# A two-layer decoder trunk: a bank of its own for the last half product, the other accumulator copied in late pairs, and the first forget weights split early with their product behind the transposes

## The chip, the cores and the metric

The kernel runs on one core of one Trainium2 chip. The metric is the device time of one execution in microseconds; lower is better. Before the change it was 1370.78 us (median of three runs, 1370.76 to 1370.94).

## The reference

A residual stream x of 1024 tokens by 1024 channels (float32) passes through two layers, and a final RMSNorm ends the trunk. Each layer is, shortened,

```python
h = rms_norm(x, norm_w[layer])
proj = h @ w_in[layer]
(q, k, v, z_attn, q_h, f_h, i_h, g_h, gate_attn, gate_hgrn) = jnp.split(proj, split_points, axis=-1)
a = sliding_window_attention(rope(q), rope(k), v, attn_sinks[layer]) * jax.nn.silu(z_attn)
logf = jnp.log(lb + (1.0 - lb) * jax.nn.sigmoid(f_h))
kin = (1.0 - lb) * jax.nn.sigmoid(-f_h)
o = hgrn2_recurrence(silu(q_h), kin, i_h, logf)
b = rms_norm_per_head(o) * jax.nn.silu(g_h)
merged = (jax.nn.sigmoid(gate_attn) * (a @ w_up_attn[layer])
          + jax.nn.sigmoid(gate_hgrn) * (b @ w_up_hgrn[layer]))
x = x + merged @ w_out[layer]
```

The attention has 8 heads of 64 channels (two key and value heads), a window of 128 tokens and one sink logit per head; the recurrence has 4 heads of 128 channels, and its forget gate is the sigmoid of f_h. Everything is float32.

## The kernel before

**Products.** A float32 product is made of three matmuls on split operands: each operand is split into a rounded high part and the rest (names hh, hl for the activations; wh or whi, wl or wlo for weights), and low by high, high by low and high by high are summed in one bank of PSUM. A weight is split by ACT (a cast, the high part) and DVE (a subtraction, the low part): `split_slot` (L463 to L472) and `split_w` (L135 to L139). PSUM has eight banks: three for the accumulators of projections and pairs (pool `pj`), five for the rest (pool `ps`, function `bank`). A matmul that opens a bank waits until the bank's last reader is done.

**Order.** Each engine runs its own queue in order, and waits for other engines through semaphores. The order within a queue is set when the kernel is built: a list scheduler takes the program's instructions and reorders them by its own estimates, unless an instruction is marked with `keep_in_program_order` or stands in a region of `manual_schedule`, where the program's order holds. The end of the last layer (function `end`) is such a region.

**The stage around the forget gate.** Attention is worked in eight blocks of 128 tokens. For step u the program calls `before(u)`, `value(u)` and `attend(u)`. `scores(b)` makes block b's scores on TensorE (tiles sc, four banks a block; ACT copies the masked half out, L837, DVE masks it, L838, and takes row maxima, L840). `softmax(b)` takes exponentials on ACT (L853, eight a block) and normalises on DVE (L856). `turn(b)` transposes the probabilities on TensorE (tiles tp, two banks of four transposes a block, L865); ACT copies each (L869) and DVE multiplies each by a mask (L870), both into pT. `values` multiplies pT by the values (tiles av, L889) for two blocks at a time; every one of these matmuls is made to wait (`wait_too`) for the DVE copies of both blocks. ACT copies av out (L882). After block 7's `value`, `forget(0, ...)` computes head 0 of the forget projection in two halves of 512 tokens, H0 and H1: 24 matmuls each into a bank of `pj` (tiles pj_f, L148 to L150, function `proj3`), and then two sigmoids and two scalings on ACT (L776 and L778), for which ACT loads another function table, and two DMAs from ACT's queue. In program order the forget product of H0 comes behind block 6's scores and ahead of block 7's, and that of H1 behind the transposes of blocks 4 and 5.

**Pairs.** `pair` makes two column groups of the input projection at once from half products, in the accumulators A, B and C. Fifteen pairs are made in each layer. For the last ones (three in the first layer, four in the second) there is no first product p1 from an earlier stage, and results are copied out of a bank by ACT and completed by sums on DVE.

**The end.** The output projection of the last layer is made of seven half products, summed by DVE into x (L1372). The last one, with the operands t2 (split as w4), adds to the banks X[0] to X[3] for row blocks 4 to 7, block 7 in two halves of 256 columns. A row block is done when its final RMSNorm is: ACT squares and sums (L1374), DVE and ACT take mean and root (L1378 to L1393), DVE scales (`scaled`, L1401), or DVE multiplies by the norm's gain early (`weigh`, L1406) and ACT scales later (`scaled_weighed`, L1410), and a DMA from SP's queue stores the block's half.

Of the kernel before, what the change touches and what calls it, by code (L numbers as in the profile page):

```python
# [17 lines left out]
P = 128  # L18
# [23 lines left out]
def trunk_kernel(ctx, tc, x, positions, norm_w, w_in, attn_sinks, hgrn_norm_w, w_up_attn,  # L42
# [101 lines left out]

    def proj3(acc, terms):
        n = len(terms)
        for i, (lh, ll, rh, rl) in enumerate(terms):
            PE.matmul(acc, lhsT=ll, rhs=rh, start=i == 0, stop=False)  # L148
            PE.matmul(acc, lhsT=lh, rhs=rl, start=False, stop=False)  # L149
            PE.matmul(acc, lhsT=lh, rhs=rh, start=False, stop=i == n - 1)  # L150
# [215 lines left out]
    def pair(w, cols, parts, hT, nm, p1, use):  # L366
# [61 lines left out]
        o22 = out("22")  # L428
        if p1 is not None:
            add(o22, C, p1)  # L430
        times(B, h1[:, 0], l1[:, 0], part(2), False)
        if p1 is not None:
            add(o22, B, o22)
        else:
            S.copy(o22, B)  # L435
            add(o22, C, o22)
        use(1, 1, o22, True)
# [10 lines left out]

    def colsA(wh, wl, hT, nm, use, groups):

        for a, o, n in groups:
            acc = pj.tile([P, n], F32, tag="pj", name=f"pj_{nm}_{a}_{o}")
            terms = []
            for k in range(KT):
                h, l = hT.half(a, k)
                terms.append((wh[:, k], wl[:, k], h[:, o:o + n], l[:, o:o + n]))
            proj3(acc, terms)
            use(a, slice(o, o + n), slice(a * 512 + o, a * 512 + o + n), acc)
# [144 lines left out]
    for L in range(DEPTH):  # L603
# [177 lines left out]
        def forget(h, w, groups):  # L781
            def use(a, o, t, acc):
                put(h, 0, t, acc, AF.Sigmoid, 1.0, lb[:, L, h:h + 1])
                put(h, 1, t, acc, AF.Sigmoid, -1.0, 0.0)
            colsA(w[0], w[1], hT, f"f{L}_{h}", use, groups)

# [144 lines left out]
        for u in range(NB):  # L931
            before(u)
            value(u)
            attend(u)
            if u == 5:
                w = [split_slot(load_chunk(wi, OF, f"f{L}_0"), f"f{L}_0", [P, KT, P])]
        w.append(chunk(wi, OQH, f"qh{L}_0"))
        for u in range(4):
# [426 lines left out]

        def add(acc, a, n, js=range(4), c=None, part=None):

            for j in js:
                b = 4 * a + j
                o, k = c or (0, 512)  # L1370
                xn = xns[b][:, n * 512 + o:n * 512 + o + k]
                V.tensor_tensor(out=xn, in0=acc[j][:, o:o + k], in1=xn, op=ALU.add)  # L1372
                if part is not None:
                    S.activation(junk[:, n * 512 + o:n * 512 + o + k], xn, AF.Square, scale=D ** -0.5,  # L1374
                                 accum_out=fs[:, part, b:b + 1])
# [31 lines left out]

        def scaled_weighed(b, n):
            t, _, d = piece(b, n)
            S.activation(t, t, AF.Copy, scale=fy[:, b:b + 1])  # L1410
            nc.sync.dma_start(d, t)

        def end():

            one = [slice(b, b + 1) for b in range(NB)]
            add(Y, 0, 1, part=1)
            w4 = split_a(t2, "t4")
            mean(slice(0, 4), 0, 1)
            square_root(slice(0, 4))
            root(slice(0, 4), 4)  # L1420
            for j in range(4):
                scaled(j, 0)
                add(X, 1, 1, [j], part=1)
                scaled(j, 1)
            weigh(4, 1)

            def last_product(j, o, n):
                for kp in range(2):
                    times(X[j][:, o:o + n], m22[kp], [t[:, :, o:o + n] for t in w4[kp]], j, False, kp)

            last_product(0, 0, 512)
            add(X, 1, 0, [0], part=0)
            weigh(5, 1)
            mean(one[4], 0, 1)
            square_root(one[4])
            last_product(1, 0, 512)
            add(X, 1, 0, [1], part=0)
            root(one[4], 1)
            scaled(4, 0)
            scaled_weighed(4, 1)  # L1440
            weigh(6, 1)
            mean(one[5], 0, 1)
            square_root(one[5])
            last_product(2, 0, 512)
            add(X, 1, 0, [2], part=0)
            root(one[5], 1)
            scaled(5, 0)
            scaled_weighed(5, 1)
            weigh(7, 1)
            mean(one[6], 0, 1)  # L1450
            square_root(one[6])
            last_product(3, 0, 256)
            add(X, 1, 0, [3], (0, 256), part=0)
            root(one[6], 1)
            V.tensor_tensor(out=fs[:, 1, one[7]], in0=fs[:, 0, one[7]], in1=fs[:, 1, one[7]], op=ALU.add)
            last_product(3, 256, 256)
            add(X, 1, 0, [3], (256, 256), part=2)
            scaled(6, 0)
            mean(one[7], 1, 2)
            square_root(one[7])  # L1460
            scaled_weighed(6, 1)
            root(one[7], 1)
            scaled_weighed(7, 1)
            scaled(7, 0)
# [97 lines left out]
```

## Time and profile before

| | us |
|---|---|
| median of three runs | 1370.78 |
| the profiled execution's own time | 1372.09 |
| its span, first to last instruction | 1370.3 |
| PE (TensorE) busy | 1354.8 |
| DVE (VectorE) busy | 974.3 |
| ACT (ScalarE) busy | 721.2 |

The profile is of one execution. A row of a timeline gives start, duration, engine, line, operation, what is written and read, shapes and count, and in brackets the idle time ahead of it and who ended it. Matmuls overlap: a matmul of 128x512 is shown with 0.39 us, while its successor starts 0.23 us later; so the pace is read from starts. Rows of waits give the waiting engine and line, the engine and line waited for, and total, count and longest in us.

### The profile page before, as it was taken

The page shows a single profiled execution, that of the slowest core. Times are in us where ns is not written, and L with a number is a line of the kernel's source. Part 1 is how long each engine was busy: PE and PEld are TensorE (multiplying, and loading weights), DVE is VectorE, ACT ScalarE, POOL GpSimd, SP SyncE. Part 2 cuts the span into 40 slices and gives each one's busy share as a digit, 9 for nine tenths or more (in the row PEclk, how much of TensorE's full clock was granted, in tenths as well). Part 3 has the DMA queues.
Part 4 walks back from the last instruction along what each step waited for, and adds up shares of the span by engine and source line. Part 5 has one row for each costly group of instructions (what it writes and reads, how often), then busy time and mean ns, then how long its engine had stood idle before and what let it go on. Part 6 is the DMA issues. An engine that isn't in the chain of part 4 may idle for free.

```text
span 1370.3 us, 21561 instructions
## 1 busy us (share of the span) xinstructions
PE 1354.8 (99%) x8248; PEld 1128.3 (82%) x8248; DVE 974.3 (71%) x1554; ACT 721.2 (53%) x1407; POOL 130.8 (10%) x211
## 2 busy tenths in 40 slices
PE   9999999999999999999999999999999999999997
PEld 8888888788877888888888888888887788888886
DVE  5877668843646888599758666777356388967987
ACT  7754334443786665326566333344357767552464
POOL 2000013220000011001010001122100000200100
PEclk9999999999999999999999999999999999999998
DMA  8636467876325842497255345587923376349813
GB/s 272 201 122 185 125 209 218 258 258 219 93 93 184 277 144 96 141 355 203 92 171 189 124 132 185 170 256 219 321 92 100 131 237 210 117 142 357 206 34 123
DMA packets 207559, 248.74 MB, mean 182 GB/s; under 512 B 14912, under 2 KB 141504, under 8 KB 207456
## 3 DMA queue, kind: packets, MB, share of 16 engines
q1 hardware_dynamic: 155744, 145.10, 32.9%
q0 software_dynamic: 15472, 49.43, 13.0%
q10 hardware_dynamic: 36240, 52.84, 10.7%
q8 instruction: 65, 1.06, 0.3%
q14 instruction: 38, 0.31, 0.1%
HBM read 162.12 MB, written 78.91 MB: 176 GB/s over the span
## 4 chain that ended last, share of the span: by engine, by line
PE 91%; DVE 5%; ACT 2%; DMA 1%; issue 1%; SPq 0%; ACTq 0%; DVEq 0%
PE pb L394 6%; PE pb L396 6%; PE pb L395 6%; PE pc L394 4%; PE pc L396 4%; PE pc L395 4%; PE pg L234 3%; PE pg L233 3%; PE pg L235 3%; PE pj_qh L148 2%; PE pj_f L148 2%; PE pj_f L150 2%; PE pj_qh L149 2%; PE pj_qh L150 2%; PE pj_f L149 2%; PE px L1353 2%
## 5 line engine op out<-in xcount | busy, mean ns | idle before, releaser
L137 ACT CAST whi_s<-ws 128x1024 fp32r<-128x1024 f32 x30 | 31.6, 1055 | 90.3 <-PE pc L396 90.3
L405 DVE TENSOR_TENSOR pq<-pc,pq 128x512 f32<-128x512 f32 x37 | 25.6, 691 | 62.1 <-PE pc L396 57.0
L627 ACT ACTIVATE pq<-pq 128x512 f32<-128x512 f32 x60 | 37.8, 630 | 45.3 <-DVE pq L405 43.8
L1155 POOL COPY scT<-acc 32x256 f32<-32x256 f32 x32 | 26.3, 822 | 284.3 <-DVE acc L1152 166.7
L137 ACT CAST whi_t<-ws 128x1024 fp32r<-128x1024 f32 x30 | 31.7, 1055 | 41.2 <-PE pc L396 27.3
L853 ACT ACTIVATE pr<-pr,mx 128x128 f32<-128x128 f32 x128 | 49.6, 391 | 4.1 <-DVE mx L850 3.7
L965 PE MATMUL pu_ua<-wh_a,wlo_ua 128*128 128x512 f32 x128 | 51.7, 404 | 0.0
L965 PE MATMUL pu_uh<-wh_b,wlo_uh 128*128 128x512 f32 x128 | 50.1, 391 | 0.5 <-DVE u L973 0.5
L967 PE MATMUL pu_ua<-wh_a,whi_ua 128*128 128x512 f32 x128 | 50.0, 391 | 0.0
L966 PE MATMUL pu_ua<-wl_a,whi_ua 128*128 128x512 f32 x128 | 50.0, 390 | 0.0
L967 PE MATMUL pu_uh<-wh_b,whi_uh 128*128 128x512 f32 x128 | 49.8, 389 | 0.0
L966 PE MATMUL pu_uh<-wl_b,whi_uh 128*128 128x512 f32 x128 | 49.8, 389 | 0.0
L137 ACT CAST whi_o<-wo 128x1024 fp32r<-128x1024 f32 x20 | 21.1, 1053 | 53.7 <-PE pu_uh L967 29.8
L394 PE MATMUL pb<-th,wl 128*128 128x512 f32 x120 | 47.2, 393 | 0.5 <-ACT pq L435 0.5
L394 PE MATMUL pc<-hh,wlo_t 128*128 128x512 f32 x120 | 46.9, 391 | 0.5 <-DVE pq L405 0.5
L394 PE MATMUL pb<-th,wlo_s 128*128 128x512 f32 x120 | 46.8, 390 | 0.2 <-DVE wlo_s L138 0.2
L394 PE MATMUL pb<-th,wlo_t 128*128 128x512 f32 x120 | 46.8, 390 | 0.0
L233 PE MATMUL pg<-hh,wl_p 128*128 128x512 f32 (+1 forms) x128 | 46.7, 365 | 0.0
L396 PE MATMUL pc<-hh,whi_t 128*128 128x512 f32 x120 | 46.7, 390 | 0.0
L396 PE MATMUL pb<-th,wh 128*128 128x512 f32 x120 | 46.7, 390 | 0.0
L395 PE MATMUL pb<-tl,wh 128*128 128x512 f32 x120 | 46.7, 389 | 0.0
L395 PE MATMUL pc<-hl,whi_t 128*128 128x512 f32 x120 | 46.7, 389 | 0.0
(453 smaller groups left out, 4475.2 us busy)
## 6 DMA issues: line engine op xcount, KB each, us to landing
wr<-in_w_in_dram SPq DMA_DIRECT2D x72, 512.0 KB, 4.7
gd<-pq ACTq DMA_DIRECT2D x79, 256.0 KB, 3.5
fq<-fq ACTq DMA_DIRECT2D x48, 256.0 KB, 2.9
wr_p<-in_w_in_dram SPq DMA_DIRECT2D x23, 512.0 KB, 6.3
x<-in_x_dram SPq DMA_DIRECT2D x16, 512.0 KB, 8.9
qs<-qsd POOLq DMA_DIRECT2D x16, 512.0 KB, 7.2
u<-gd SPq DMA_DIRECT2D x16, 512.0 KB, 10.2
ga<-gd SPq DMA_DIRECT2D x16, 512.0 KB, 10.6
```

The source lines that it names most:

```text
L137: S.copy(hi, raw)
L148: PE.matmul(acc, lhsT=ll, rhs=rh, start=i == 0, stop=False)
L149: PE.matmul(acc, lhsT=lh, rhs=rl, start=False, stop=False)
L150: PE.matmul(acc, lhsT=lh, rhs=rh, start=False, stop=i == n - 1)
L233: PE.matmul(acc, lhsT=wl[:, k], rhs=h[:, t], start=k == ks[0][0], stop=False, skip_group_check=q > 0)
L394: PE.matmul(acc, lhsT=wl[:, k], rhs=h, start=start and k == 0, stop=False, skip_group_check=not start)
L395: PE.matmul(acc, lhsT=wh[:, k], rhs=l, start=False, stop=False, skip_group_check=not start)
L396: PE.matmul(acc, lhsT=wh[:, k], rhs=h, start=False, stop=k == 3, skip_group_check=not start)
L853: S.activation(pr[:, h], pr[:, h], AF.Exp, bias=mx[:, h:h + 1], accum_out=sm[:, h:h + 1])
L965: PE.matmul(acc, lhsT=w[1][:, k, c], rhs=hi[:, i], start=k == 0, stop=False)
L966: PE.matmul(acc, lhsT=w[0][:, k, c], rhs=lo[:, i], start=False, stop=False)
L967: PE.matmul(acc, lhsT=w[0][:, k, c], rhs=hi[:, i], start=False, stop=k == 3)
```

## The change

Three parts.

1. In `end`, the last half product's right half of block 7 gets a bank of its own, Z, and starts it new; what was in the right half of X[3] before is added to x by a sum of its own ahead of it. The split of t2 stands first, five of the first eight `scaled` stand ahead of the sums, the `weigh` of blocks 4 to 6 are grouped, root and scale of a block change places with the sum of the next, and the last `scaled_weighed` issues its DMA from ACT's queue.
2. In `pair`, where there is no p1, ACT copies accumulator C as soon as it is done, and DVE adds B to the copy; before, ACT copied B and DVE added C.
3. The load and split of the first forget weights stand ahead of `attend(5)`, and the first matmul of each half of `forget(0, ...)` is kept in program order.

```diff
-    def proj3(acc, terms):
+    def proj3(acc, terms, pin=False):
         n = len(terms)
         for i, (lh, ll, rh, rl) in enumerate(terms):
-            PE.matmul(acc, lhsT=ll, rhs=rh, start=i == 0, stop=False)
+            mm = PE.matmul(acc, lhsT=ll, rhs=rh, start=i == 0, stop=False)
+            if pin and i == 0:
+                tc.keep_in_program_order(mm)
...
         o22 = out("22")
-        if p1 is not None:
-            add(o22, C, p1)
+        first(o22, C)
         times(B, h1[:, 0], l1[:, 0], part(2), False)
-        if p1 is not None:
-            add(o22, B, o22)
-        else:
-            S.copy(o22, B)
-            add(o22, C, o22)
+        add(o22, B, o22)
...
-            colsA(w[0], w[1], hT, f"f{L}_{h}", use, groups)
+            colsA(w[0], w[1], hT, f"f{L}_{h}", use, groups, h == 0)
...
             value(u)
-            attend(u)
             if u == 5:
                 w = [split_slot(load_chunk(wi, OF, f"f{L}_0"), f"f{L}_0", [P, KT, P])]
+            attend(u)
...
+            w4 = split_a(t2, "t4")
             add(Y, 0, 1, part=1)
-            w4 = split_a(t2, "t4")
...
+            add(X, 1, 0, [3], (256, 256))
+            Z = bank([P, 256], f"pz_{L}")
...
-            last_product(3, 0, 256)
+            last_product(X[3][:, 0:256], 3, 0, 256)
             add(X, 1, 0, [3], (0, 256), part=0)
+            mean_root(6)
+            last_product(Z, 3, 256, 256, True)
+            V.tensor_tensor(out=fs[:, 1, one[7]], in0=fs[:, 0, one[7]], in1=fs[:, 1, one[7]], op=ALU.add)
             root(one[6], 1)
-            V.tensor_tensor(out=fs[:, 1, one[7]], in0=fs[:, 0, one[7]], in1=fs[:, 1, one[7]], op=ALU.add)
-            last_product(3, 256, 256)
-            add(X, 1, 0, [3], (256, 256), part=2)
+            scaled_weighed(6, 1)
+            add([None] * 3 + [Z], 1, 0, [3], (256, 256), part=2, at=0)
             scaled(6, 0)
-            mean(one[7], 1, 2)
-            square_root(one[7])
-            scaled_weighed(6, 1)
+            mean_root(7, 1, 2)
             root(one[7], 1)
-            scaled_weighed(7, 1)
+            scaled_weighed(7, 1, nc.scalar)
             scaled(7, 0)
```

How the queues change. First TensorE's, first layer, from the transposes of blocks 2 and 3 (tp_2, tp_3) on; pj_f_0_0 is the forget product of H0, av_2 the values of block 2. Before:

```order
L865 MATMUL tp_2_0_3347<-ident,pr_2_3012 128x128 x4
L148 MATMUL pj_f_0_0_0_3486<-hh_0_0_172,wl_f_0_3267 128x512
L149 MATMUL pj_f_0_0_0_3486<-hl_0_0_180,wh_f_0_3266 128x512
...
L865 MATMUL tp_2_1_3355<-ident,pr_2_3012 128x128 x4
L865 MATMUL tp_3_0_3363<-ident,pr_3_3089 128x128 x4
L865 MATMUL tp_3_1_3371<-ident,pr_3_3089 128x128 x4
L150 MATMUL pj_f_0_0_0_3486<-hh_0_0_172,wh_f_0_3266 128x512
...
L148 MATMUL pj_f_0_0_0_3486<-hh_0_3_175,wl_f_0_3267 128x512
L889 MATMUL av_2_3407<-pT_2_0_3352,vn_2604 64x256 x2
```

and now (line numbers are those of the changed kernel):

```order
L862 MATMUL tp_2_0_3347<-ident,pr_2_3012 128x128 x4
L862 MATMUL tp_2_1_3355<-ident,pr_2_3012 128x128 x4
L862 MATMUL tp_3_0_3363<-ident,pr_3_3089 128x128 x4
L862 MATMUL tp_3_1_3371<-ident,pr_3_3089 128x128 x4
L886 MATMUL av_2_3407<-pT_2_0_3352,vn_2604 64x256 x2
...
L148 MATMUL pj_f_0_0_0_3486<-hh_0_0_172,wl_f_0_3198 128x512
L151 MATMUL pj_f_0_0_0_3486<-hl_0_0_180,wh_f_0_3197 128x512
```

Before, 5 matmuls of the forget product stood behind the first four transposes and 17 behind the others, ahead of av_2. Now av_2 follows the transposes directly, and all 24 stand behind block 6's scores. Next TensorE's queue at the transposes of blocks 4 and 5, with pj_f_0_1, the forget product of H1. Before:

```order
L833 MATMUL sc_7_1_1_3537<-ks_1_0_2805,qs_3_1_2815 128x256
L148 MATMUL pj_f_0_1_0_3600<-hhi_0_2797,wl_f_0_3267 128x512
L865 MATMUL tp_4_0_3568<-ident,pr_4_3216 128x128 x4
L149 MATMUL pj_f_0_1_0_3600<-hlo_0_2801,wh_f_0_3266 128x512
...
L150 MATMUL pj_f_0_1_0_3600<-hh_1_3_179,wh_f_0_3266 128x512
L865 MATMUL tp_4_1_3576<-ident,pr_4_3216 128x128 x4
```

and now:

```order
L830 MATMUL sc_7_1_1_3537<-ks_1_0_2805,qs_3_1_2815 128x256
L862 MATMUL tp_4_0_3568<-ident,pr_4_3222 128x128 x4
L862 MATMUL tp_4_1_3576<-ident,pr_4_3222 128x128 x4
L862 MATMUL tp_5_0_3584<-ident,pr_5_3299 128x128 x4
L862 MATMUL tp_5_1_3592<-ident,pr_5_3299 128x128 x4
L148 MATMUL pj_f_0_1_0_3600<-hhi_0_2797,wl_f_0_3198 128x512
```

The 23 forget matmuls between the first four transposes of block 4 and the next ones stand behind all of them now. Last, ACT's queue at the forget gate (fq is its result, pr_6 the probabilities of block 6, pr_7 those of block 7). Before:

```order
L837 COPY pr_6_3432<-sc_6_1_1_3449 128x2x128
L853 ACTIVATE pr_5_3299,sm_5_3464<-pr_5_3299,mx_5_3298 128x128 x3
L776 ACT_TABLE_LOAD
L776 ACTIVATE fq_0_0_0_3511<-pj_f_0_0_0_3486 128x512
...
L837 COPY pr_7_3520<-sc_7_0_0_3521 128x2x128
```

and now:

```order
L834 COPY pr_6_3432<-sc_6_1_1_3449 128x2x128
L848 ACTIVATE es_6_3553<-es_6_3553 128x8
L850 ACTIVATE pr_6_3432,sm_6_3552<-pr_6_3432,mx_6_3431 128x128 x6
L773 ACT_TABLE_LOAD
L773 ACTIVATE fq_0_0_0_3511<-pj_f_0_0_0_3486 128x512
...
L834 COPY pr_7_3520<-sc_7_0_0_3521 128x2x128
```

Six exponentials of block 6 stand ahead of the table load now, where three of block 5 stood, and the copies of block 7's scores stay behind the gate's activations. In the second layer the same orders stand.

More of the change, by code (lines that the diff above doesn't have):

```diff
@@ L447, in pair, with colsA @@
             use(1, 0, B, False)
-    def colsA(wh, wl, hT, nm, use, groups):
+    def colsA(wh, wl, hT, nm, use, groups, pin=False):
         for a, o, n in groups:
@@ L456, in colsA @@
                 terms.append((wh[:, k], wl[:, k], h[:, o:o + n], l[:, o:o + n]))
-            proj3(acc, terms)
+            proj3(acc, terms, pin)
             use(a, slice(o, o + n), slice(a * 512 + o, a * 512 + o + n), acc)
@@ L1364, in trunk_kernel, with add @@
             fm, ft, fy = (st.tile([P, NB], F32, tag=f"f{n}", name=f"f{n}", bufs=1) for n in "mty")
-        def add(acc, a, n, js=range(4), c=None, part=None):
+        def add(acc, a, n, js=range(4), c=None, part=None, at=None):
             for j in js:
@@ L1371, in add @@
                 xn = xns[b][:, n * 512 + o:n * 512 + o + k]
-                V.tensor_tensor(out=xn, in0=acc[j][:, o:o + k], in1=xn, op=ALU.add)
+                V.tensor_tensor(out=xn, in0=acc[j][:, (o if at is None else at):][:, :k], in1=xn, op=ALU.add)
                 if part is not None:
@@ L1406, in weigh, with scaled_weighed, last_product, mean_root @@
             V.tensor_tensor(out=t, in0=t, in1=w, op=ALU.mult)
-        def scaled_weighed(b, n):
+        def scaled_weighed(b, n, queue=nc.sync):
             t, _, d = piece(b, n)
             S.activation(t, t, AF.Copy, scale=fy[:, b:b + 1])
-            nc.sync.dma_start(d, t)
+            queue.dma_start(d, t)
         def end():
             one = [slice(b, b + 1) for b in range(NB)]
+            def last_product(acc, j, o, n, start=False):
+                for kp in range(2):
+                    times(acc, m22[kp], [t[:, :, o:o + n] for t in w4[kp]], j, start, kp)
+            def mean_root(b, i=0, j=1):
+                mean(one[b], i, j)
+                square_root(one[b])
+            w4 = split_a(t2, "t4")
             add(Y, 0, 1, part=1)
-            w4 = split_a(t2, "t4")
             mean(slice(0, 4), 0, 1)
@@ L1420, in end @@
             root(slice(0, 4), 4)
+            todo = [(b, n) for b in range(4) for n in range(2)]
+            for b, n in todo[:5]:
+                scaled(b, n)
             for j in range(4):
-                scaled(j, 0)
                 add(X, 1, 1, [j], part=1)
[L1424 to L1429, printed above, removed]
@@ L1431, in end @@
-            last_product(0, 0, 512)
-            add(X, 1, 0, [0], part=0)
[L1433 to L1436, printed above, removed]
-            add(X, 1, 0, [1], part=0)
[L1438 to L1444, printed above, removed]
+                for b, n in todo[5 + j:6 + j]:
+                    scaled(b, n)
@@ new lines, in end @@
+            add(X, 1, 0, [3], (256, 256))
+            Z = bank([P, 256], f"pz_{L}")
+            last_product(X[0], 0, 0, 512)
+            for b in (4, 5, 6):
+                weigh(b, 1)
+            add(X, 1, 0, [0], part=0)
+            weigh(7, 1)
+            mean_root(4)
+            last_product(X[1], 1, 0, 512)
+            root(one[4], 1)
+            scaled_weighed(4, 1)
+            scaled(4, 0)
+            add(X, 1, 0, [1], part=0)
+            mean_root(5)
+            last_product(X[2], 2, 0, 512)
@@ L1445, in end @@
+            root(one[5], 1)
+            scaled_weighed(5, 1)
             add(X, 1, 0, [2], part=0)
-            root(one[5], 1)
             scaled(5, 0)
[L1448 to L1451, printed above, removed]
-            last_product(3, 0, 256)
+            last_product(X[3][:, 0:256], 3, 0, 256)
             add(X, 1, 0, [3], (0, 256), part=0)
+            mean_root(6)
+            last_product(Z, 3, 256, 256, True)
+            V.tensor_tensor(out=fs[:, 1, one[7]], in0=fs[:, 0, one[7]], in1=fs[:, 1, one[7]], op=ALU.add)
```

## The prediction

> **What bounds the kernel now.** I read the page's busy times and the chain that ended last first.
>
> ```profile
> span 1370.3 us, 21561 instructions
> PE 1354.8 (99%) x8248; PEld 1128.3 (82%) x8248; DVE 974.3 (71%) x1554; ACT 721.2 (53%) x1407; POOL 130.8 (10%) x211
> ...
> PE 91%; DVE 5%; ACT 2%; DMA 1%; issue 1%; SPq 0%; ACTq 0%; DVEq 0%
> ```
>
> TensorE is at work for all but 15 us of the span, so a microsecond in which it waits is a microsecond of the result, and work of DVE or ACT costs only where TensorE stands for it. The view of waits, for TensorE, shows what the change can win:
>
> ```profile
> PE px L1353 <- DVE x L1372: 1.7, 1, 1.7
> ...
> PE pj_f L148 <- DVE wl_f L471: 0.9, 2, 0.4
> ...
> PE pb L394 <- ACT pq L435: 0.5, 1, 0.5
> ```
>
> These three rows are its three parts: the last half product (1.7 us, once), the first forget product (0.4 us in each layer) and the late pairs (0.5 us, once). All together some 3 us. What it can lose lies in how TensorE's queue is rearranged, above all around the forget product. The timeline of TensorE there, first layer:
>
> ```profile
> 370.08 0.66 PE L865 MATMUL tp<-ident,pr 128*128 128x128 f32 x4
> 371.18 0.50 PE L148 MATMUL pj_f<-hh,wl_f 128*128 128x512 f32 x1 [0.44 <-DVE wl_f L471]
> ...
> 372.44 1.47 PE L865 MATMUL tp<-ident,pr 128*128 128x128 f32 x12
> 373.67 0.48 PE L150 MATMUL pj_f<-hh,wh_f 128*128 128x512 f32 x1
> ...
> 377.42 0.39 PE L148 MATMUL pj_f<-hh,wl_f 128*128 128x512 f32 x1
> 377.74 0.65 PE L889 MATMUL av<-pT,vn 128*64 128x256 f32 x4
> ...
> 383.35 0.40 PE L149 MATMUL pj_f<-hl,wh_f 128*128 128x512 f32 x1
> ...
> 383.82 0.28 PE L829 MATMUL sc<-ks,qs 128*128 128x256 f32 x1
> ...
> 385.72 0.40 PE L148 MATMUL pj_f<-hhi,wl_f 128*128 128x512 f32 x1
> 385.96 0.60 PE L865 MATMUL tp<-ident,pr 128*128 128x128 f32 x4
> 386.31 0.47 PE L149 MATMUL pj_f<-hlo,wh_f 128*128 128x512 f32 x1
> ```
>
> The first column is the start; starts give the pace: 16 forget matmuls from 373.67 to 377.42, 0.23 us each; 12 transposes in 1.23 us, 0.10 each. Between the transposes of the probabilities of blocks 2 and 3 (tp) and the products that use them (av) stand 22 forget matmuls, and 23 more between the first and the other transposes of blocks 4 and 5. They are what TensorE does while DVE and ACT copy the transposes out.
>
> **The change, part by part.**
>
> *Forget product, first stall.* The split moves ahead of attend(5). DVE is free there, so this costs nothing:
>
> ```profile
> 367.86 1.25 DVE L838 COPY_PREDICATED pr<-upper,sc 128x256 f32<-128x256 int32 x3 [4.50 <-ACT pr L837]
> ...
> 369.92 1.21 DVE L471 TENSOR_TENSOR wl_f<-wr_f,wh_f 128x1024 fp32r<-128x1024 f32 x1
> 371.05 0.68 DVE L840 TENSOR_REDUCE mx<-pr 128x4 f32<-128x512 f32 x1
> ...
> 375.65 1.28 DVE L870 TENSOR_TENSOR pT<-tp,side 128x512 f32<-128x512 f32 x2
> ```
>
> The 4.50 us of idle before 367.86 take the 1.21. The stall goes: the four transposes from 370.08 need 0.41, the matmul came at 371.18, so 0.7 us per layer. And DVE's queue, which has no idle from 367.86 to 376.93, loses the 1.13 between 369.92 and 371.05: its last copy (pT of block 3) ends at 375.8.
>
> But the pin holds the whole product behind block 6's scores. TensorE now runs 16 transposes at 0.10, from 370.08 to 371.8, and then stands before av_2, which waits for that last copy: 375.9 − 371.8 = 4.1 us; I take 4.0. The bounds are 3.5 (transposes 0.5 late for their banks) and 4.3. The 22 matmuls (5 us) that covered this are not saved, they follow later.
>
> *Second stall.* From av_2 to the end of block 6's scores took 377.74 to 383.35, 5.6 us: now 375.9 to 381.5. Then 24 forget matmuls at 0.23 (5.5) to 387.0, 16 scores of block 7 (383.82 to 385.72, 1.9) to 388.9, four transposes to 389.3. The next four need the bank of block 7's first scores, so ACT's copy and DVE's mask of it. On ACT that copy stands behind the forget gate's activations:
>
> ```profile
> 375.10 0.40 ACT L853 ACTIVATE pr<-pr,mx 128x128 f32<-128x128 f32 x1 [0.36 <-DVE mx L850]
> ...
> 385.25 1.28 ACT L776 ACT_TABLE_LOAD   x1
> 386.54 1.09 ACT L776 ACTIVATE fq<-pj_f 128x512 f32<-128x512 f32 x2
> ...
> 389.34 1.20 ACT L837 COPY pr<-sc 128x256 f32<-128x256 f32 x4 [0.40 <-ACT fq L778]
> ```
>
> ```profile
> 383.04 1.25 DVE L838 COPY_PREDICATED pr<-upper,sc 128x256 f32<-128x256 int32 x3 [3.05 <-ACT pr L837]
> ...
> 386.06 0.17 DVE L841 TENSOR_TENSOR mx<-mx,sink 128x8 f32<-128x8 f32 x1
> ...
> 389.75 1.11 DVE L838 COPY_PREDICATED pr<-upper,sc 128x256 f32<-128x256 int32 x3 [2.06 <-ACT pr L837]
> ```
>
> From the table load to the first copy are 4.1 us, to DVE's mask 0.4 more, and the mask itself lasts 0.4. In the new order six exponentials of block 6 stand ahead of the load. They need DVE's maxima of block 6. The exponentials began at 375.10, behind DVE, so now at 374.0; the sixteen of blocks 4 and 5 at 0.39 and two copies of av at 0.5 last to 381.2; DVE normalises block 5 (1.2) to 382.5, and masks and maxima (3.0 from 383.04 to 386.06) with the small steps behind them (0.4) end at about 386.0. Six exponentials then end at 388.3, so the bank is free at 388.3 + 4.1 + 0.8 = 393.2. Stall: 393.2 − 389.3 = 3.9; I take 3.8. Were the exponentials never in the way, the activations would still wait for the product's end at 387.0: 2.8 from activation to copy (386.54 to 389.34) and 0.8 give 390.6, a stall of 1.3. The upper bound is 4.2. Before, 23 matmuls lay there, from 386.31 on.
>
> Per layer 4.0 + 3.8 − 0.7 = 7.1; the bounds are 4.1 (3.5 + 1.3 − 0.7) and 7.8 (4.3 + 4.2 − 0.7). For two layers **+14.2** (8.2 to 15.6).
>
> *The clock after a stall.* The kernel has one longer stall of TensorE, 1.8 us near the end. Its windows (length, busy of PE, PEld, DVE, ACT, POOL, then granted clock):
>
> ```profile
> 1360.00:1361.80 1.80, 0.08 (x2) 0.01 (x1) 1.80 (x5) 1.01 (x4) 0.00 (x0) 1.00 0.26 96
> 1361.80:1363.00 1.20, 1.20 (x10) 1.20 (x11) 0.63 (x4) 0.51 (x2) 0.00 (x0) 1.00 0.99 370
> 1363.00:1363.20 0.20, 0.20 (x4) 0.20 (x3) 0.00 (x0) 0.00 (x0) 0.00 (x0) 0.75 0.08 21
> 1363.20:1363.70 0.50, 0.50 (x3) 0.21 (x1) 0.00 (x0) 0.00 (x0) 0.00 (x0) 0.50 0.00 0
> ```
>
> After work had resumed at 1361.80 the clock fell to 0.50 at about 1363.1. Four stalls of near 4 us would each do this. How long it lasts the start shows (first matmuls, PE only):
>
> ```profile
> 1.00:2.50 1.50, 1.45 (x7) 1.00 0.40 21
> ...
> 5.50:7.00 1.50, 1.50 (x14) 1.00 0.85 252
> ```
>
> Seven matmuls in 1.5 us, later fourteen: half pace (the clock column has no record yet), which ended between 4.0 and 5.5, some 3.5 us after the first. Such a spell costs 1.75 us if TensorE works throughout it, less where part of it falls in the stall. I take 1.2 for each of four, **+4.8** (0 to 7.0).
> The Trainium skill ("TensorE: Matmul & The Clock Gate", Part 1) says the same more sharply: a free-running window of 3.4 us with TensorE idle halves the clock, and a busy one restores it. It speaks against this change; by it the stalls of 3.8 and 4.0 us are long enough to be caught and the term would be near 4 × 1.7 = 6.8, an estimate; the fall after only 1.8 us in the trace says that a window half idle is enough.
>
> *Pairs without p1* (three in the first layer, four in the second). ACT copies accumulator C instead of B, DVE adds B instead of C: as many instructions of the same shapes. What was on the path is one wait:
>
> ```profile
> 937.55 0.39 PE L394 MATMUL pb<-hh,wlo_a 128*128 128x512 f32 x1
> ...
> 937.75 0.59 ACT L435 COPY pq<-pb 128x512 f32<-128x512 f32 x1 [1.66 <-PE pb L396]
> ...
> 938.39 0.50 PE L394 MATMUL pb<-th,wl 128*128 128x512 f32 x1 [0.45 <-ACT pq L435]
> ```
>
> A matmul due at 937.78 came at 938.39: 0.6, and 0.1 of restart, so **−0.7**. The copy of C now has the 12 matmuls of B (2.7 us) as cover, and DVE's sum of B the next 12. If ACT were 2.2 us behind (0.59 of the 2.7 is the copy itself) TensorE would wait. Bounds −0.8 and +1.4 (0.2 in each of seven).
>
> *The end.*
>
> ```profile
> 1361.32 0.42 DVE L1372 TENSOR_TENSOR x<-px,x 128x256 f32<-128x256 f32 x1
> ...
> 1362.18 0.16 DVE L1393 SCALAR_TENSOR_TENSOR fy<-ft,fy 128x1 f32<-128x1 f32 x1
> ...
> 1363.74 0.42 DVE L1372 TENSOR_TENSOR x<-px,x 128x256 f32<-128x256 f32 x1 [1.21 <-PE px L1356]
> ```
>
> The right half waited for the left half's sum (1361.32), since both lay in one bank: the 1.8 us of the first window above. With its own bank it follows at once, and the sum of it, 1363.74 before, could start at about 1361.9. Now DVE is last: the left half's sum can start near 1360.2, when its product is done; fy of block 6 came 0.9 after that start (1362.18), and now ACT's square of the half, some 0.6, and its root lie between, so it comes at about 1362.1 and the bank's sum at 1362.2, 1.5 ahead of 1363.74. ACT then scales block 6 ahead of its square of the right half, which costs 0.2 to 0.3 of that; the last store has one issue fewer ahead of it on SP, since block 7's other half goes from ACT's queue, some 0.4. I take **−1.6**. Bounds: −0.3 (DVE, with one more sum of 0.42 and 1.2 of idle at 1363.74 to give up, stays as late as before) and −2.3 (the whole 1.8 and the issue).
>
> **The sum**: 14.2 + 4.8 − 0.7 − 1.6 = +16.7. The profiled execution took 1372.09 for its span of 1370.3; the runs shown have a median of 1370.78, and 16.7 on that is **1387.5**.
>
> **The rivals.**
> *The clock holds*, or its spells fall inside the stalls: 14.2 − 2.3 = +11.9, 1382.7. For it: no stall of 4 us is in this trace; against it: the fall after 1.8.
> *The second stall is short* (1.3, no fall there): per layer 4.0 + 1.3 − 0.7 = 4.6; twice, with two spells of 1.2 and −2.3 from pairs and end: +9.3, 1380.1. It needs DVE to finish block 6's maxima 2.5 earlier than I count.
> *Everything stretches*: stalls at 15.6, spells at 7.0, the pairs' copies late at 1.4, the end at −0.3: +23.7, 1394.5.
> *The faster side: the copies out of the transposes are done in time.* It is decided at av_2: if DVE's last copy for block 3 were there by 371.8 and not 375.8, the matmuls taken away covered nothing, the second stall shrinks likewise, and what is left are −1.4 for wl_f, −0.7 and −1.6: −3.7, 1367.1. Against it stands DVE's row at 375.65, with no idle ahead of it since 367.86; it would need 4 us of DVE work to go where the change takes 1.13. The gains of 3.7 are used up once the two stalls together are 1.9 per layer.
> *The pin does not do what it says*: then the forget matmuls would still be among the transposes; the new queue shows that they are not.
>
> **How the numbers follow.** Forecast 0.55, clock holds 0.20, short second stall 0.10, everything stretches 0.07, faster 0.05, and 0.03 for stalls so small that gains and losses cancel. A measurement of this kernel tells 0.2% (2.7 us) from no change. Slower: 0.55 + 0.20 + 0.10 + 0.07 = 0.92. The range runs from 1375.9 (stalls at 8.2, no fall, best pairs and end: +5.1) to 1392, short of the stretched case, and leaves out no more than two in ten.
>
> **What would show it.** In the waits of the changed kernel, av L886 behind DVE's pT with near 4 us, twice, and tp L862 behind DVE's mask pr with near 4 us, twice; no wait for wl_f, none for pq in the pairs, none for px; the clock under 1.00 in the windows after each stall. A TensorE wait at av_2 under 2 us would break the main step; a clock of 1.00 behind stalls of 4 us would break the second.

## The result, and the profile after

The changed kernel is slower: 1393.20 us (median of five executions, 1389.99 to 1394.62) beside 1370.94 us for the kernel before, run next to it (1370.76 to 1372.03). The ratio is 1.0156, with a 95% interval of 1.0145 to 1.0167. In all experiments together, two executions stand far off (4848.69 us of the kernel before, 3521.01 us of the early split alone) and no figure below counts them. The forecast was 1387.5 with a range of 1375.9 to 1392.0: the direction and the main mechanism came true, and the time lies 1.2 us above the range.

The profiled execution is the fastest of the five, 1389.99 us for a span of 1388.2. The page's busy times and its chain of waits, of the changed kernel:

```profile
span 1388.2 us, 21567 instructions
PE 1359.1 (98%) x8248; PEld 1132.0 (82%) x8248; DVE 972.8 (70%) x1555; ACT 718.9 (52%) x1407; POOL 129.7 (9%) x211
...
PE 80%; DVE 11%; DMA 3%; ACT 2%; issue 2%; SPq 1%; POOL 0%; ACTq 0%; DVEq 0%
```

The count of matmuls is the same, 8248, and the span is 17.9 longer. TensorE's part of the chain fell from 91% to 80%, DVE's rose from 5% to 11%. TensorE's waits, changed kernel (engine and line, the one waited for, total us, count, longest):

```profile
PE av L886 <- DVE pT L867: 7.4, 4, 3.4
PE tp L862 <- DVE pr L835: 5.3, 2, 2.7
PE lv L1074 <- issue: 3.2, 2, 1.7
```

The three waits that the change was to remove (px, pj_f for wl_f, pb for pq) are gone. The first two rows are the two stalls that were forecast. The third was not: lv, the first products of the recurrence.

The two stalls in the first layer, in the timelines of TensorE, ACT and DVE of the changed kernel:

```profile
370.61 1.09 PE L862 MATMUL tp<-ident,pr 128*128 128x128 f32 x8 [0.15 <-DVE mx L838]
...
373.79 1.28 DVE L867 TENSOR_TENSOR pT<-tp,side 128x512 f32<-128x512 f32 x2
...
375.13 1.12 PE L886 MATMUL av<-pT,vn 128*64 128x256 f32 x4 [3.42 <-DVE pT L867]
...
380.28 0.50 PE L826 MATMUL sc<-ks,qs 128*128 128x256 f32 x2
...
381.98 1.24 DVE L835 COPY_PREDICATED pr<-upper,sc 128x256 f32<-128x256 int32 x3 [0.20 <-ACT pr L834]
...
385.31 0.21 ACT L848 ACTIVATE es<-es 128x8 f32<-128x8 f32 x1 [2.29 <-DVE es L846]
...
387.95 1.28 ACT L773 ACT_TABLE_LOAD   x1
389.25 1.08 ACT L773 ACTIVATE fq<-pj_f 128x512 f32<-128x512 f32 x2
...
389.67 0.60 PE L862 MATMUL tp<-ident,pr 128*128 128x128 f32 x4
...
392.03 1.20 ACT L834 COPY pr<-sc 128x256 f32<-128x256 f32 x4 [0.40 <-ACT fq L775]
...
392.44 1.11 DVE L835 COPY_PREDICATED pr<-upper,sc 128x256 f32<-128x256 int32 x3 [6.96 <-ACT pr L834]
...
392.94 1.53 PE L862 MATMUL tp<-ident,pr 128*128 128x128 f32 x12 [2.67 <-DVE pr L835]
```

TensorE has its last transpose of block 3 done at 371.7, DVE its last copy at 375.07, and av_2 starts right behind that. The 32 av then take 5.15 us (375.13 to 380.28), where they take 3.6 at full pace (the kernel with filled stalls, below). Later TensorE stands before tp_4_1 until ACT has done the gate's activations, copied block 7's scores, and DVE has masked them: 392.03, 392.44, 392.94, in that order.

The granted clock around both stalls, in windows of the changed kernel (length, busy of PE, PEld, DVE, ACT, POOL, then clock, DMA share, GB/s):

```profile
371.70:375.10 3.40, 0.01 (x1) 0.00 (x0) 3.40 (x10) 2.81 (x13) 0.00 (x0) 0.97 0.14 53
375.10:378.50 3.40, 3.37 (x18) 1.98 (x20) 1.81 (x5) 3.40 (x20) 0.00 (x0) 0.53 0.00 0
378.50:382.00 3.50, 3.50 (x32) 2.66 (x29) 1.61 (x4) 2.59 (x10) 0.00 (x0) 1.00 0.28 80
390.00:393.00 3.00, 0.33 (x4) 0.10 (x3) 0.56 (x2) 2.60 (x7) 0.78 (x1) 1.00 0.38 141
393.00:396.50 3.50, 3.50 (x22) 3.13 (x23) 3.20 (x10) 3.47 (x9) 0.00 (x0) 1.00 0.08 29
```

Behind the first stall the clock is halved for some 3.2 us; behind the second it stays at 1.00. The second layer repeats both (0.58 in 1058.1 to 1061.5, 1.00 in 1075.8 to 1079).

**Where the 17.9 us came from.** I took the start of the same matmuls in both traces and followed the difference. It is +0.24 from the first 20 us on, before any change, −0.7 at the transposes of block 2 (the pairs' gain, first layer) and +6.9 when the stage is over and the query product of head 1 begins: the stage cost 7.6. It is +8.6 behind the first lv and l of head 0, and +9.75 at the layer's end. In the second layer the pairs bring it to 8.7 at the transposes of block 2; the stage costs 7.4, lv 1.6 more, the rest of the recurrence 1.5, and from 1180 on it stands at 19.2. The end takes back 1.3. The sum: stages 15.0, lv 3.3, later recurrence 2.6, pairs −2.0, end −1.3 and the 0.24 of the start, which is 17.9 but for rounding.

### The profile page after: what moved, and what is told of

Same layout as the page of the kernel before. It is cut to its first block, busy times and chain, and to the rows that moved or that the text cites. A ratio compares the mean times of both kernels' runs of the same rounds, so it can differ in the third digit from the quotient of the medians.

```text
span 1388.2 us, 21567 instructions
## 1 busy us (share of the span) xinstructions
PE 1359.1 (98%) x8248; PEld 1132.0 (82%) x8248; DVE 972.8 (70%) x1555; ACT 718.9 (52%) x1407; POOL 129.7 (9%) x211
## 4 chain that ended last, share of the span: by engine, by line
PE 80%; DVE 11%; DMA 3%; ACT 2%; issue 2%; SPq 1%; POOL 0%; ACTq 0%; DVEq 0%
PE pb L396 6%; PE pb L398 6%; PE pb L397 6%; PE pc L396 4%; PE pc L398 4%; PE pc L397 4%; PE pg L235 3%; PE pg L237 3%; PE pg L236 3%; PE av L886 2%; PE pu_uh L962 2%; PE pu_uh L963 2%; PE pu_uh L964 2%; PE pi L913 2%; PE pi L912 2%; PE pi L914 2%
## 5 line engine op out<-in xcount | busy, mean ns | idle before, releaser
L407 DVE TENSOR_TENSOR pq<-pc,pq 128x512 f32<-128x512 f32 x30 | 20.7, 690 | 47.8 <-PE pc L398 47.8
L397 PE MATMUL pb<-tl,whi_s 128*128 128x512 f32 x120 | 46.7, 389 | 0.0
L398 PE MATMUL pb<-th,whi_s 128*128 128x512 f32 x120 | 46.7, 389 | 0.0
L396 PE MATMUL pc<-th,wlo_s 128*128 128x512 f32 x120 | 46.7, 389 | 0.0
```

Of the source, the lines that this page charges most:

```text
L396: PE.matmul(acc, lhsT=wl[:, k], rhs=h, start=start and k == 0, stop=False, skip_group_check=not start)
L397: PE.matmul(acc, lhsT=wh[:, k], rhs=l, start=False, stop=False, skip_group_check=not start)
L398: PE.matmul(acc, lhsT=wh[:, k], rhs=h, start=False, stop=k == 3, skip_group_check=not start)
```

## The experiments

Every ratio is against runs of the kernel before beside them; that kernel's medians in these sessions lay between 1371.25 and 1372.26.

### All but the pin

```diff
-            mm = PE.matmul(acc, lhsT=ll, rhs=rh, start=i == 0, stop=False)
-            if pin and i == 0:
-                tc.keep_in_program_order(mm)
+            PE.matmul(acc, lhsT=ll, rhs=rh, start=i == 0, stop=False)
...
-            colsA(w[0], w[1], hT, f"f{L}_{h}", use, groups, h == 0)
+            colsA(w[0], w[1], hT, f"f{L}_{h}", use, groups)
```

> The change without the pin (first forget matmul free again; tail, pairs and early split kept). Theory, the pin's stalls are the whole loss: the gains seen in the changed kernel stay, 1.3 at the end, 2.6 in the pairs, and 1.4 for the two waits on wl_f: 1370.9 - 5.3 = 1365.6, with no wait of av or tp over 0.5 us. Rival, the early split (or the pairs) moves the queues as well: near 1390.

Measured: 1372.4, ratio 1.0007 (0.9998 to 1.0016). Without the pin there is no stall at av or tp, so the pin carries nearly all of the slowdown, some 21 us. But it was to be faster than before and is not; its waits show a new one at lv, as in the changed kernel, though at head 2 (494.6 us in the first layer) and not at head 0:

```profile
PE lv L1072 <- issue: 4.1, 2, 2.0
```

### The pin alone

```diff
-            PE.matmul(acc, lhsT=ll, rhs=rh, start=i == 0, stop=False)
+            mm = PE.matmul(acc, lhsT=ll, rhs=rh, start=i == 0, stop=False)
+            if pin and i == 0:
+                tc.keep_in_program_order(mm)
...
-            colsA(w[0], w[1], hT, f"f{L}_{h}", use, groups)
+            colsA(w[0], w[1], hT, f"f{L}_{h}", use, groups, h == 0)
```

> Only the pin (the first forget matmul of each half kept in program order), split as before. Theory, the pin alone makes the loss and the other parts only win: 1393.2 + 1.3 (end) + 2.6 (pairs) = 1397, some more if wl_f lengthens DVE's queue ahead of av_2 (up to 1.1 in each layer): 1397 to 1400. Rival, pin and early split only cost together: under 1385.

Measured: 1397.0 (1394.86 to 1399.46), ratio 1.0186 (1.0171 to 1.0202), as expected. The pin's two stalls are there as in the changed kernel, with the late pairs, the old end and the old split beside them:

```profile
PE av L891 <- DVE pT L872: 7.2, 4, 3.3
PE tp L867 <- DVE pr L840: 5.4, 2, 2.7
PE tp L867 <- DVE mx L843: 2.8, 2, 1.4
```

The third row is new: with the split in its old place, the transposes behind the first four wait 1.4 us in each layer for their bank, where the changed kernel waits 0.15. DVE splits wl_f (369.90, 1.21 us) among block 3's maxima here, and 7 us ahead of them (362.56) in the changed kernel.

### The pin on one half only

First the pin on H0 alone, with the rest of the change:

```diff
-            proj3(acc, terms, pin)
+            proj3(acc, terms, pin and a == 0)
```

> The whole change with the pin on the first half H0 alone; 19 matmuls of the second half stand again between the transposes of block 4. Theory: the stall at av_2 (3.6) and its spell of slow clock (1.6) stay in each layer, the stall at the transposes of block 4 (2.8) goes and the wait of lv (1.8) shrinks: 1365.6 + 2 x 5.2 = 1376, to 1378. Rival, each pin costs half: 1379.5. Rival, the second stall is the one that matters: under 1372.

Then on H1 alone (`a == 1` in the same place):

> The whole change with the pin on the second half H1 alone; 20 matmuls of the first half stand again ahead of av_2. Theory: the stall at the transposes of block 4 (2.8) and the wait of lv (1.8) stay, the stall at av_2 goes: 1365.6 + 2 x 4.6 = 1375, up to 1378 where the clock falls behind the stall. Rival, the second stall was only there because the first had delayed ACT: under 1370.

Measured: H0 alone 1383.57, ratio 1.0086 (1.0073 to 1.0098); H1 alone 1387.95 (1384.52 to 1389.88), ratio 1.0117 (1.0101 to 1.0132). Over the kernel without a pin that is, by the medians, +11.2 and +15.6, 26.8 together, where both pins cost 20.8. The expectations (1376 to 1378, and 1375 to 1378) stood on 1365.6 for the kernel without a pin, which took 1372.4. Over that, H0 costs what was expected (10.4 to 12.4) and H1 more (9.2 to 12.4 was expected). Each pin makes one of the stalls, as expected. With H0 alone it is again 3.42 long, and the halved clock and the recurrence behind it add to it. With H1 alone the second stall is not 2.7 but 4.1, and this one does halve the clock, for longer than the first stall did. TensorE's timeline and the clock windows of the kernel with H1 pinned:

```profile
388.84 2.82 PE L862 MATMUL tp<-ident,pr 128*128 128x128 f32 x12 [4.13 <-DVE pr L835]
...
394.02 0.63 PE L148 MATMUL pj_f<-hhi,wl_f 128*128 128x512 f32 x1
394.45 0.53 PE L151 MATMUL pj_f<-hlo,wh_f 128*128 128x512 f32 x1
394.81 0.40 PE L152 MATMUL pj_f<-hhi,wh_f 128*128 128x512 f32 x1
```

```profile
385.00:388.80 3.80, 0.00 (x0) 0.00 (x0) 1.70 (x5) 3.39 (x9) 0.21 (x1) 0.88 0.27 100
388.80:391.30 2.50, 2.46 (x12) 2.46 (x13) 2.43 (x6) 2.47 (x8) 0.00 (x0) 0.50 0.16 57
391.30:394.60 3.30, 3.30 (x10) 2.62 (x9) 1.09 (x5) 3.30 (x17) 0.00 (x0) 0.50 0.00 0
394.60:398.00 3.40, 3.40 (x16) 2.81 (x15) 3.23 (x5) 3.38 (x15) 0.00 (x0) 0.98 0.00 0
```

Half pace from 388.8 to 394.6: the 12 transposes take 2.5 us for 1.2, and eight matmuls 3.5 for 1.8, so the spell costs some 2.9, and stall and spell 7.0 per layer. So the stalls are not independent: take the first away and the second grows. TensorE has block 4's first four transposes 5.6 us earlier than in the changed kernel (384.10 for 389.67), and the chain of ACT and DVE that frees block 7's bank ends only 4.1 earlier (388.84 for 392.94), although no exponential of block 6 stands ahead of ACT's table load here, where six stand in the changed kernel.

### The stalls filled with work

This kernel is the changed one with matmuls added whose result nothing reads: 14 ahead of av_2 and 11 ahead of tp_4_1, in each layer. It computes all that the changed kernel does.

```diff
+        def fill(n, nm):
+            acc = pj.tile([P, 512], F32, tag="pj", name=f"pj_fill_{L}_{nm}")
+            h, _ = hT.half(0, 0)
+            for i in range(n):
+                mm = PE.matmul(acc, lhsT=w[0][0][:, 0], rhs=h, start=True, stop=True)
+                wait_too(mm, turned_last[0])
+                tc.keep_in_program_order(mm)
...
+                if b == 4 and g == 1:
+                    fill(11, 1)
...
+            if u == 7:
+                fill(14, 0)
```

> The whole change, with matmuls whose result nobody reads put into both stalls of each layer: 14 (3.2 us) between the transposes of block 3 and av_2, 11 (2.5 us) behind the first four transposes of block 4. No wait is shortened by them. Theory, slow clock behind the stalls costs 1.6 per spell, two spells in the profiled execution and more in the others: the granted clock stays at 1.00 there, the time falls to 1386 to 1388 and its spread (1390.0 to 1394.6) shrinks to under 1 us. Rival, the clock costs nothing and the stalls are all: 1393, or more by the matmuls that do not fit.

Measured: 1389.18 (1388.46 to 1391.31), ratio 1.0132 (1.0118 to 1.0145), 4.0 less than the changed kernel's median (3.3 by the two ratios). Timeline of this kernel, TensorE and ACT:

```profile
370.65 3.45 PE L934 MATMUL pj_fill<-hh,wh_f 128*128 128x512 f32 x14
374.32 0.65 PE L888 MATMUL av<-pT,vn 128*64 128x256 f32 x4 [0.22 <-DVE pT L869]
...
384.09 0.21 ACT L848 ACTIVATE es<-es 128x8 f32<-128x8 f32 x1 [2.27 <-DVE es L846]
384.30 0.40 ACT L850 ACTIVATE pr<-pr,mx 128x128 f32<-128x128 f32 x1
...
384.70 0.39 ACT L850 ACTIVATE pr<-pr,mx 128x128 f32<-128x128 f32 x1
...
385.20 1.28 ACT L773 ACT_TABLE_LOAD   x1
...
387.67 2.77 PE L934 MATMUL pj_fill<-hh,wh_f 128*128 128x512 f32 x11
...
432.25 0.64 PE L1088 MATMUL lv<-f,ones 128*32 128x256 f32 x8 [2.67 <-issue]
```

With TensorE busy, av runs at full pace (32 of them from 374.32 to 377.93), the granted clock is 1.00 behind both stalls in both layers, and the profiled execution's mean clock is 0.999 for 0.996. So the halved clock comes of the idle time.

That the time is won by the clock is not shown, for the scheduler gave ACT another order as well: between block 6's maxima and the table load stand two exponentials of block 6 here (384.30 and 384.70) and six in the changed kernel (from 385.31 to 387.95), in both layers. Four fewer at 0.39 us are 1.5 us of the chain that frees block 7's bank. From the transposes of block 2 to the query product of head 1 the filled kernel is 1.9 us shorter in the first layer and 1.8 in the second; 1.5 of each goes by ACT's order, and 0.3 to 0.4 are left for the clock.

In the first layer of the profiled execution even that is used up: the kernel is 2.7 ahead at the query product of head 1 (0.8 of it from before the stage), 1.8 behind the lv of head 0, where the wait grew from 1.72 to 2.67, and level at 485 us, behind two waits of 0.68 us at po. In the second layer the gain stays, and the spans differ by 1.5 (1386.7 and 1388.2), the medians by 4.0. The time is above the expected 1388, and the spread of 2.9 is larger than the expected 1.

### The end alone, and the pairs alone

The end alone is the whole of the first part; two of its lines:

```diff
+            Z = bank([P, 256], f"pz_{L}")
...
+            last_product(Z, 3, 256, 256, True)
```

> Only the end changed. Theory: -1.3 (what the changed kernel wins behind its last marks) to the predicted -1.6: 1369.3 to 1369.6. Rival, DVE stays last there: 1370.9, no difference.

```diff
-        if p1 is not None:
-            add(o22, C, p1)
+        first(o22, C)
...
-        else:
-            S.copy(o22, B)
-            add(o22, C, o22)
+        add(o22, B, o22)
```

> Only the pairs without p1 changed. Theory, from the ledger of the changed kernel (-1.2 and -1.3 between the pair stages' marks): -2.6, 1368.3. Rival, the prediction's term of one removed wait: -0.7, 1370.2.

Measured: the end 1370.48, ratio 0.9989 (0.9980 to 0.9998), some −1.5; the pairs 1370.16, ratio 0.9990 (0.9981 to 0.9999), some −1.4. The first is what was expected. The second lies between theory and rival, and its interval (−0.1 to −2.6) takes in both; the changed kernel's trace has −2.0.

### The early split alone

```diff
-            attend(u)
             if u == 5:
                 w = [split_slot(load_chunk(wi, OF, f"f{L}_0"), f"f{L}_0", [P, KT, P])]
+            attend(u)
```

> Only the load and split of the first forget weights moved ahead, no pin. Theory: the two waits on wl_f go, -1.4, 1369.5, and the forget matmuls still stand among the transposes. Rival, the early split opens the wait of av behind pT: +7 or more, 1378 and above.

Measured: 1375.3, ratio 1.0024 (1.0015 to 1.0034): +3.3, where −1.4 was expected. The wait for wl_f is gone, and 0.8 us are won by it in each layer. They are lost again, and more, at lv and l of head 2, some 110 us behind the edit: 2.3 us in the first layer, 3.3 in the second. The wait in the view, and DVE's timeline there, of the kernel with the early split:

```profile
PE lv L1077 <- issue: 4.1, 2, 2.0
```

```profile
479.89 0.69 DVE L1031 TENSOR_TENSOR Q<-Q,tab 128x512 f32<-128x512 f32 x1 [3.44 <-PE l L1129]
...
483.94 1.21 DVE L1052 TENSOR_TENSOR gs<-R,Q 128x1024 f32<-128x1024 f32 x1
```

and of the kernel before:

```profile
477.54 1.22 DVE L1052 TENSOR_TENSOR gs<-R,Q 128x1024 f32<-128x1024 f32 x1 [2.79 <-DMA Q<-fq]
```

Part of the second layer's loss is the clock. Its wait of 2.04 us at lv was followed by half the granted clock, the first layer's of 2.03 was not (windows of the kernel with the early split, with columns as above):

```profile
495.00:498.50 3.50, 3.46 (x95) 2.78 (x96) 3.50 (x5) 0.46 (x2) 0.00 (x0) 1.00 0.37 96
1170.60:1174.00 3.40, 3.40 (x88) 2.50 (x79) 3.40 (x7) 0.80 (x3) 0.00 (x0) 0.50 0.49 137
```

gs is where the chain of a head begins on DVE. Before, it starts when its data come, at 477.5. With the early split the list scheduler has put head 1's last step, which waits for TensorE, and the root of head 0's norm ahead of it, and it starts at 483.9.

On SP's queue, too, a load of weights moved ahead of head 2's loads. To tell the two apart, that load alone was held back:

```diff
-            w = up_chunk(w_up_attn[L], m, f"ua{L}_{m}")
+            w = up_chunk(w_up_attn[L], m, f"ua{L}_{m}", fetched[2].ins if m == 4 else None)
...
-                nc.sync.dma_start(d, fqd[h][n])
+                fetched[h] = nc.sync.dma_start(d, fqd[h][n])
```

> Only the early split, as in the run of the split alone, with one load (the third block of the attention projection) held behind the loads of head 2's gates and query on SP's queue, as the order before had it; DVE's order stays that of the early split. Theory, DVE's order (head 2's chain behind a step of head 1 that waits for TensorE) makes the wait of lv: no change, ratio 1.002 to 1.003. Rival, the load ahead on SP's queue makes head 2 late: the wait of lv goes and the 1.4 of wl_f is left, ratio 0.999.

Measured: 1374.98, ratio 1.0028 (1.0017 to 1.0039). The load is not the cause. A further kernel does the reverse: the kernel before, with no early split and only DVE's order changed.

```diff
-            V.tensor_tensor(out=gs, in0=R, in1=Q, op=ALU.mult)
+            with tc.issue_after(rooted[0].ins) if h == 2 else ExitStack():
+                V.tensor_tensor(out=gs, in0=R, in1=Q, op=ALU.mult)
...
-            V.tensor_tensor(out=ot, in0=ot, in1=ro.unsqueeze(2).broadcast_to([P, NB, P]), op=ALU.mult)
+            rooted[h] = V.tensor_tensor(out=ot, in0=ot, in1=ro.unsqueeze(2).broadcast_to([P, NB, P]), op=ALU.mult)
```

> The kernel before, with one order changed and nothing else asked for: VectorE's first product of the recurrence's head 2 (gs, and with it the chain behind it) is held behind the root of head 0's norm, as it came to stand with the early split. No early split, no pin, the old pairs and end. Theory (the early split alone costs its 3.3 us because head 2's chain on VectorE starts some 6 us later, behind head 1's last step): the same loss shows without any split, waits of lv on TensorE of near 2 us in each layer and a time of 4 to 5 us above the kernel before (the 1.4 that the split saves elsewhere are not there), near 1375 to 1376.5. Rival (the loss comes from something else that the early split moves, the load on SP or the banks): the kernel is within 1 us of the kernel before, and no lv wait shows.

Measured: 1376.95 (1375.71 to 1377.86), ratio 1.0036 (1.0023 to 1.0050): +4.9. The size is as the theory has it, the place is not: no wait at lv is in the view, but one of the same length at the products beside it. Waits of TensorE and DVE's timeline of this kernel:

```profile
PE pu_ua L965 <- DVE wlo_ua L138: 4.4, 2, 2.3
```

```profile
481.29 0.17 DVE L117 TENSOR_SCALAR ms_o<-so 128x8 f32<-128x8 f32 x1 [6.76 <-ACT f L1202]
...
486.45 1.41 DVE L1055 TENSOR_TENSOR gs<-R,Q 128x1024 f32<-128x1024 f32 x1
```

DVE is idle for 6.76 us here and 6.96 (3.52 and 3.44) with the early split, against 2.79 before. It then has everything to do at once, and TensorE waits for whichever piece stands last: lv in the one order, the split of the next weights (wlo_ua) in the other. That asking for this one order of DVE costs this much is shown. TensorE's queue changed with it (six of the pu_ua products stand ahead of lv where none stood), and in the first layer the clock fell behind the wait (0.51 from 496.9 to 500.3): the loss is 3.8 us there and 2.2 in the second layer, where it did not fall. That the whole 3.3 of the early split (with the 1.5 won at wl_f, 4.8) come from DVE's order is the likely reading, since the two orders are alike but not the same.

### The parts that gain

```diff
-            if u == 5:
-                w = [split_slot(load_chunk(wi, OF, f"f{L}_0"), f"f{L}_0", [P, KT, P])]
             attend(u)
+            if u == 5:
+                w = [split_slot(load_chunk(wi, OF, f"f{L}_0"), f"f{L}_0", [P, KT, P])]
```

This is the changed kernel without the pin and with the split in its old place: the end and the pairs alone.

> The end and the pairs changed, forget weights and forget product as before (no early split, no pin). Theory, the gains add: ratios 0.9989 x 0.9990 = 0.9979, some 2.9 us under the kernel before, 1368.4 on 1371.3. Rival, part of the pairs' gain is eaten further on: 0.999.

Measured: 1368.97 (1368.24 to 1370.28), ratio 0.9983 (0.9974 to 0.9992). It is faster than the kernel before by some 2.3 us, and than the changed one by 24; the interval takes in both the theory and the rival. It also accounts for the kernel without the pin: 0.9983 with these parts and 1.0024 with the early split give 1.0007, which is what was measured there.

## Why the prediction was right and where it was wrong

**The first stall** was forecast as 4.0, with a bound of 3.5 if the transposes came 0.5 late for their banks. That is what happened: they took 2.3 us for 1.7, and the stall was 3.4 to 3.6. DVE's last copy ended at 375.07; the kernel is 0.7 earlier there than before, so that is 375.8 by the forecast's clock, as forecast.

**The second stall** was forecast as 3.8 and measured 2.7 to 2.8. Its end was nearly right: the bank was forecast free at 393.2, and the transposes came at 392.94, 393.65 by the forecast's clock. What was wrong is when TensorE arrived: at 390.1, 390.8 by that clock, and not at 389.3, since its av had run at half pace. From the pin on H1 the same is seen from the other side: TensorE comes without the first stall, and waits 4.1. The six exponentials stood in the way for the reason given, DVE's maxima of block 6, which were done at 385.48, 386.2 by the forecast's clock, for the forecast 386.0.

**The clock** was added as a term of its own, 1.2 behind each of four stalls. Here the step failed. In the profiled execution only two stalls were followed by a halved clock, and those two spells (1.55 and 1.4 us of TensorE's time) lie inside a stretch whose end ACT and DVE set. DVE was normalising block 5 until 381.79 and then waited only 0.20 us for block 6's scores (the row at 381.98), so the later scores moved that end by no more than this; the spells shortened the second stall instead of adding to it. Stalls and clock together were forecast as 19.0 (14.2 and 4.8), and the two stages took 15.0.

**The cost behind the stage** was priced at nothing, and this is the step that carried the time out of the range. The sum ended with the transposes. But when they are late, the products behind them are late too, and with them the recurrence's chain over ACT, SP's load and DVE. ACT's last gate activation of head 0 waits for TensorE and starts 2.3 us later than before (416.51 for 414.22), and gs, the chain's first step on DVE, 2.8:

```profile
423.31 1.23 DVE L1052 TENSOR_TENSOR gs<-R,Q 128x1024 f32<-128x1024 f32 x1 [6.29 <-DMA Q<-fq]
```

in the kernel before, and in the changed one

```profile
426.12 1.22 DVE L1049 TENSOR_TENSOR gs<-R,Q 128x1024 f32<-128x1024 f32 x1 [6.82 <-DMA Q<-fq]
...
433.25 0.69 DVE L1037 TENSOR_TENSOR R<-R,tab 128x512 f32<-128x512 f32 x1
434.03 0.64 PE L1074 MATMUL lv<-f,ones 128*32 128x256 f32 x8 [1.72 <-issue]
```

The view names no engine for the wait of lv, but its operand R is done at 433.94, just ahead. From gs to that row's end DVE takes 7.8 us in both kernels. In the kernel before, TensorE had 33 matmuls of the next query product ahead of lv and met it without a wait (431.72, with R done at 431.14); now five stand there, and it waits 1.7 to 1.9. The lateness alone would not have made it wait: 28 more matmuls are 6.3 us, more than the wait. It takes the scheduler's new order too, and no run separates the two. lv is 3.3 us in the two layers; with the 2.6 that follow in the recurrence that is 5.9 us in the profiled execution, for nothing in the forecast. What filled the 2.6, small waits at po, u and l, was not taken apart.

**The median against the profiled execution.** The profiled execution by itself, 1389.99, lies in the range; the other four lie 2.6 to 4.6 above it, with mean clocks of 0.993 to 0.994 for its 0.996. A mean clock lower by 0.0025 (the means are given to 0.001) is 0.0025 × 1390 / 0.5 = 7 us more at half clock: two spells of the length seen, as many as there are second stalls. That would be a second stall that halves the clock in these executions and does not in the profiled one. The kernel with the pin alone speaks against it: its profiled execution, with a mean clock of 0.997, took 1397.82, and three others with 0.993 took 1396.85 to 1399.46. No profile of a slower execution of the changed kernel exists, and why the median lies 3.2 above the profiled execution stays open.

**Pairs and end** were forecast as −0.7 and −1.6. The end gives −1.3 in the trace and −1.5 alone. The pairs give −2.0 in the trace and −1.4 alone, past the bound of −0.8. The step that failed is "what was on the path is one wait". The view of the kernel before has a second one of the same length in the late pairs, at 245.44 in the first layer, under another name:

```profile
PE pc L394 <- DVE pq L405: 0.5, 1, 0.5
```

It is gone in the changed kernel and with the pairs alone.

**The split that "costs nothing".** In its own place that was true: DVE's idle time took it, and the wait for wl_f went, for 0.8 us per layer with the split alone (0.7 was forecast). But an instruction moved in a scheduled program moves others, and alone it makes the kernel 3.3 us slower, most likely through DVE's order 110 us later. Under the pin that order is not there (the changed kernel keeps head 2's gs ahead of head 1's last step), so this did not add to the miss; it did decide that the change without the pin gains nothing.

**The rivals.** "The faster side" was decided where it was said, at av_2, by DVE's copies. "The clock holds" (1382.7) is refuted by the windows at 0.53. Its other half, that the spells fall inside the stalls, is near to what the stages show, 15.0 for its 14.2; its time is too low mainly by the 5.9 behind the stage. "The second stall is short" counted 1.3 with DVE early; it was 2.7, with DVE on time and TensorE late. "Everything stretches" had the nearest time, 1394.5, but by other terms: stalls longer and pairs late, neither of which came.

## What to carry to other kernels

Independent work that stands between an operation and its consumer is cover, and its worth is read from the other engine's end time: DVE's last copy and ACT's copies set when the consumer can start, whatever TensorE does. Stalls that end at times set by other engines can't be added up, nor can a slower clock in between be added to them where such an engine sets the end; what can be added is only the time at which the last of them ends, and then the next chain behind it must be followed until the lateness is used up. Where a scheduler orders the queues, a moved instruction should be judged by comparing every engine's order to the end of the program, not only around the edit; this holds for an experiment that adds work to one queue as well.

## What the runs showed of the hardware

The length of a stall does not by itself tell whether the clock falls. In these profiles TensorE's next matmuls ran at half pace for 2.7 to 3.2 us after idle times of 3.32, 3.42 and 3.43 us, and for 5.2 to 5.8 us after 4.13; after 2.67 and 2.72 they kept their pace. But the clock fell after shorter idle times too: after 1.8 us near the end of the kernel before, after 2.11 us in the kernel with only DVE's order changed, and after 2.04 us in the second layer of the early split alone, where 2.03 us in the first layer left it at 1.00. In the kernel with H0 pinned it fell to 0.50 from 479.0 to 482.4 behind two waits of 0.68 us at po. By the windows, the clock stood at 0.50 for 3.4 us behind the stalls up to 3.43 (374.9 to 378.3 in the changed kernel) and for 6.8 us behind 4.13 (387.9 to 394.7 with H1 pinned), some of it within the stall. The Trainium skill ("TensorE: Matmul & The Clock Gate", Part 1) gives an idle window of about 3.4 us for the fall and a busy one of the same length for the return. The spells of 3.4 us and the kept pace after 2.7 agree with it; the falls behind 0.68 to 2.1 us of idle came sooner than it says, and the spell of 6.8 us lasted longer than one such window.

TensorE work whose result nobody reads can hold the clock at 1.00 through a stall: the windows show it for 25 such matmuls in each layer. What that is worth in time was not shown here, since ACT's order changed with it.
